# The opening of the first feed-forward product in a two-layer trunk: four sums instead of five, other work moved behind them

## The chip, the cores and the metric

The kernel runs on one core of one Trainium2 chip. The metric is device microseconds of one execution. Of the kernel before, three runs are known: 1134.08, 1134.33 and 1135.26 us, median 1134.33 us. One more execution was profiled: 1136.75 us, of which 1135.0 us are the profiled span and 1.75 us lie around it. Engines are called as the profile calls them: PE (TensorE matmuls), DVE (VectorE), ACT (ScalarE), POOL (GpSimd) and SP (SyncE, which issues most transfers).

## The reference

The input x has 512 tokens of 1024 features. Two layers follow, then a last normalization:

```python
h = rmsnorm(x, attn_norm[l])
proj = einsum('bsd,de->bse', h, w_in[l])        # 1024 -> 3072
... stick-breaking attention on one half, differential attention on the other ...
x = x + einsum('bse,ed->bsd', mixed, w_o[l])    # 1024 -> 1024
h = rmsnorm(x, mlp_norm[l])
u = square(relu(einsum('bsd,df->bsf', h, w_ff1[l])))   # 1024 -> 4096
x = x + einsum('bsf,fd->bsd', u, w_ff2[l])             # 4096 -> 1024
```

All is float32. The change lies mainly in `einsum(h, w_ff1[l])`, the first feed-forward product.

## The kernel before, in words

**Split numbers.** Every float32 operand of a product is split into a high part that TensorE takes exactly (ACT copies it with rounding: `whi`, `h_hi`, `T_hi`, `Ah`) and a low part, the rest (DVE subtracts: `wlo`, `h_lo`, `T_lo`, `Al`). A product is three matmuls: high by high, high by low, low by high (`three`, lines 289 to 294). So each weight tile of 128x1024 costs one ACT and one DVE instruction ("a split", lines 127 and 128), and each is used by 24 matmuls of 256 columns in the feed-forward stage.

**Feed-forward stage.** Each layer has four groups of 1024 of the 4096 hidden features. For both products a group uses a scheme with seven block products in place of eight. In the first product the blocks of h are two halves of the features by two halves of the tokens (`lo_t`, `hi_t`). The seven kinds are taken in the order `1, 2, 5, 6, 7, 3, 4` (`HALVES`), each for two column blocks c = 0, 1. Kinds 1, 2 and 3 use h as it is. Kinds 5, 6, 7 and 4 use sums of h's blocks. These four sums are made once per layer by `opening` (lines 852 to 866), in place in the two scaled copies of h (`hxs`), and split into `T_hi` and `T_lo`. All four groups use them.

The weights of kinds 5, 6, 7 and 3 are sums too. They are made partly by DMAs that add onto a tile, and partly on DVE by `sum1` (line 827, rows named `q<-q,q`), the "raw sums": "y" before kind 6, "z" before kind 3.

**PSUM.** Kinds 1, 6, 7 and 4 of a column block go one after the other into one bank (spot "a"), each added onto what stands there; kinds 5 and 3 share another ("b"). So before kind 7 starts to add, ACT must have copied the bank after kind 6 (`F`, line 949), and before kind 4, after kind 7 (line 951). `tap` makes these copies, adds on DVE (lines 946, 952, 957), and "bends" the finished hidden features: relu and square, two ACT instructions each (line 941), put off until the next product has been issued.

**Second product.** Its seven forms (`11, 21, x1, ...`) use the hidden features of the group and sums of them. `roll` splits one: `Ah` on ACT, `Al` on DVE. The first is rolled ("11") behind kind 2, the next ("21") behind kind 4.

**What sets the order.** A scheduler places instructions on each engine, but a chain of manual dependencies (`line`) fixes the order of the listed ACT and DVE instructions as written, for the feed-forward stage. Each engine works in order, so an instruction that waits holds all behind it. `W.next` takes the split tile for the next 24 matmuls and calls for the splits of the tiles up to five ahead. In the attention stage there are only two split tiles in turn, besides a few "homes": tiles in memory that is not yet used, into which some weights can be split early (`at_home`).

**Start of a layer.** Layer 0 begins with the projections d0, d1, w0, d2, d3 and so on. The sum of squares for the norm goes through a reduction (`ms`), a power on POOL (`rcol`) and a broadcast by PE (`rb_a`). Two homes held the weights of d2 (units 6 and 7) in layer 0.

Of the kernel before, what the change touches and what calls it, by code (L numbers as in the profile page):

```python
# [13 lines left out]
ALU = mybir.AluOpType  # L14
# [157 lines left out]
def trunk(ctx, tc, xT, w, w1, w2, gains, gfin, lamv, cos, sin, out):  # L172
    nc = tc.nc
# [115 lines left out]
    def three(pt, a, b, first, last, onto=False):  # L289
        ah, al = a  # L290
        bh, bl = b
        nc.tensor.matmul(pt, ah, bh, start=first, stop=False, skip_group_check=onto)  # L292
        nc.tensor.matmul(pt, ah, bl, start=False, stop=False, skip_group_check=onto)  # L293
        nc.tensor.matmul(pt, al, bh, start=False, stop=last, skip_group_check=onto)  # L294
# [33 lines left out]
    for l in range(L):  # L328
        last = l == L - 1
        with ExitStack() as actx:  # L330
# [25 lines left out]
            if l == 0:  # L356
# [17 lines left out]
                at_home(6, vs_parts)  # L374
            else:
# [5 lines left out]
                for n in (1, 2):  # L381
                    W.do_split(W.used + n)
                    behind(W.last[1], h[1])
# [6 lines left out]
                W.gate = W.used + 6, squares[-1][1], behind  # L390

# [457 lines left out]
            def t_part(k, t):  # L849
                split(T_hi[:, 4 * k : 4 * k + 4, t], T_lo[:, 4 * k : 4 * k + 4, t], hxs[k][:, :, t])  # L850

            def opening(n):
                b12, b11, b22, b21 = (hxs[k][:, :, t] for k in range(2) for t in (lo_t, hi_t))
                if n == 0:
                    nc.vector.tensor_sub(b11, b11, b12)
                    t_part(0, hi_t)
                elif n == 1:
                    nc.vector.tensor_sub(b21, b22, b21)
                    nc.vector.tensor_sub(b12, b22, b12)
                    nc.vector.scalar_tensor_tensor(  # L860
                        out=b22, in0=b22, scalar=-1.0, in1=b11, op0=ALU.mult, op1=ALU.subtract)
                    t_part(1, lo_t)
                elif n == 2:
                    t_part(0, lo_t)
                elif n == 3:
                    nc.vector.tensor_add(b21, b21, b11)
                    t_part(1, hi_t)
# [12 lines left out]
            for g in range(GROUPS):  # L880
                for c in range(GP // 2):
                    then("q", g, "5", c, sum1, "y", g, c)
                    then("q", g, "6", c, sum1, "z", g, c)
# [24 lines left out]
        with ExitStack() as fctx:  # L908
# [163 lines left out]
            for g in range(GROUPS):  # L1072
                end = g == GROUPS - 1
                kinds = iter(("s", "s", "s", "mm", "mm", "o"))
                for q in HALVES:
                    for c in range(GP // 2):
                        if g == 0:
                            opening({("1", 0): 1, ("2", 0): 2, ("2", 1): 3}.get((q, c)))
# [6 lines left out]
                        for i in range(2):  # L1085
                            for cc in range(4):
                                three(pt[:, 256 * i : 256 * i + 256], wpair(u, 4 * i + cc), mover(q, cc),
                                      q in "125" and i == cc == 0, i == 1 and cc == 3, q not in "125")
# [158 lines left out]
```

## Time and profile before

| what | value |
| --- | --- |
| runs, median (lowest to highest) | 1134.33 us (1134.08 to 1135.26) |
| profiled execution: its time, its span | 1136.75 us, 1135.0 us |
| granted TensorE clock, mean | 0.994 |
| PE busy | 98% of the span |
| DVE busy | 82% |
| ACT busy | 63% |
| POOL busy | 15% |
| DMA | 162 GB/s mean |

A row of the timeline gives the start of an instruction in us, its duration, the engine, the line, the operation, what it writes and reads with sizes, and in brackets the idle time before it and what ended it. The row of a wait gives the total, the number of times and the longest. Rows of a stretch give busy time per engine (instructions), the granted clock (PEclk) and the DMA's share. Matmuls are pipelined: a start follows the one before by less than the duration shown.

### The profile page before, as it was taken

How to read it: one execution, taken by the hardware profiler on the slowest of the kernel's cores; microseconds unless marked ns; L12 is line 12 of the kernel's file. 1: busy time of each engine (PE TensorE's matmuls, PEld its weight loads, DVE VectorE, ACT ScalarE, POOL GpSimd, SP SyncE). 2: the span in 40 equal slices, each digit the busy share in tenths (PEclk: the TensorE clock that was granted, in tenths of full speed). 3: DMA queues.
4: the chain of work that ended last, by engine and by line, in shares of the span. 5: the costliest groups of instructions: out<-in, count | busy, mean ns of one | idle time of the engine just before them, and what ended most of it. 6: DMA issues, size and time to landing. Idle time of an engine off the chain costs nothing.

```text
span 1135.0 us, 18049 instructions
## 1 busy us (share of the span) xinstructions
PE 1116.2 (98%) x6834; PEld 998.1 (88%) x6834; DVE 929.2 (82%) x1238; ACT 711.1 (63%) x1120; POOL 174.5 (15%) x257
## 2 busy tenths in 40 slices
PE   9999999998999999999999999999999999999997
PEld 6889989898889899899888898888988998998986
DVE  7898778897788887878888876887977888878787
ACT  7456666676667566567545566665676666565575
POOL 0001432110210110111100024231101101102012
PEclk9999999998999999999999999999999999999999
DMA  7664453255887876885645743524577777859766
GB/s 257 198 173 125 113 148 101 84 151 174 181 189 201 169 194 211 173 212 139 126 130 155 192 118 112 159 83 136 107 226 162 170 222 161 204 155 194 178 128 151
DMA packets 60471, 183.39 MB, mean 162 GB/s; under 512 B 7521, under 2 KB 8545, under 8 KB 60385
## 3 DMA queue, kind: packets, MB, share of 16 engines
q1 hardware_dynamic: 46272, 131.62, 36.6%
q0 software_dynamic: 13824, 50.34, 25.2%
q8 instruction: 54, 0.88, 0.3%
q10 hardware_dynamic: 288, 0.28, 0.1%
q14 instruction: 33, 0.26, 0.1%
HBM read 154.95 MB, written 2.10 MB: 138 GB/s over the span
## 4 chain that ended last, share of the span: by engine, by line
PE 83%; DVE 8%; ACT 3%; DMA 2%; issue 2%; POOL 1%; SPq 0%; POOLq 0%; ACTq 0%; DVEq 0%
PE f L292 8%; PE f L293 8%; PE f L294 8%; PE x L294 2%; PE x L293 2%; PE x L292 2%; DVE wlo L128 2%; PE wo L292 2%; PE wo L293 2%; PE wo L294 2%; DMA q<-in_w 1%; ACT whi L127 1%; DMA raw<-in_w 1%; PE T0s L591 1%; PE T1s L591 1%
## 5 line engine op out<-in xcount | busy, mean ns | idle before, releaser
L128 DVE TENSOR_TENSOR wlo<-q,whi 128x1024 fp32r<-128x1024 f32 x184 | 223.5, 1220 | 24.9 <-ACT whi L127 24.4
L127 ACT ACTIVATE whi<-q 128x1024 fp32r<-128x1024 f32 x184 | 190.3, 1052 | 51.3 <-DMA q<-in_w 23.8
L292 PE MATMUL f<-T_hi,whi 128*128 128x256 f32 x512 | 147.6, 288 | 6.1 <-ACT F L949 6.1
L293 PE MATMUL f<-T_lo,whi 128*128 128x256 f32 x512 | 146.7, 286 | 0.0
L294 PE MATMUL f<-T_hi,wlo 128*128 128x256 f32 x512 | 146.6, 286 | 0.0
L841 POOL DMA_DIRECT2D q<-in_w x64 | 56.2, 912 | 374.1 <-DVE wlo L128 354.2
L292 PE MATMUL f<-h_hi,whi 128*128 128x256 f32 x384 | 108.9, 284 | 0.6 <-ACT whi L127 0.6
L293 PE MATMUL f<-h_lo,whi 128*128 128x256 f32 x384 | 108.7, 283 | 0.0
L294 PE MATMUL f<-h_hi,wlo 128*128 128x256 f32 x384 | 108.6, 283 | 0.0
L292 PEld LDWEIGHTS f<-T_hi,whi 128*128 128x128 f32 x512 | 100.1, 196 | 6.5 <-ACT F L949 6.5
L293 PEld LDWEIGHTS f<-T_lo,whi 128*128 128x128 f32 x512 | 100.1, 196 | 0.0
L294 PEld LDWEIGHTS f<-T_hi,wlo 128*128 128x128 f32 x512 | 100.1, 196 | 0.0
L941 ACT ACTIVATE F<-F 128x512 f32<-128x512 f32 x112 | 70.4, 628 | 21.8 <-DVE F L946 19.8
L128 DVE TENSOR_TENSOR wlo<-raw,whi 128x1024 fp32r<-128x1024 f32 (+1 forms) x62 | 72.1, 1173 | 4.7 <-ACT whi L127 4.7
L292 PEld LDWEIGHTS f<-h_hi,whi 128*128 128x128 f32 x384 | 73.7, 192 | 1.3 <-ACT whi L127 1.0
L293 PEld LDWEIGHTS f<-h_lo,whi 128*128 128x128 f32 x384 | 73.7, 192 | 0.3
L294 PEld LDWEIGHTS f<-h_hi,wlo 128*128 128x128 f32 x384 | 73.7, 192 | 0.1
L127 ACT ACTIVATE whi<-raw 128x1024 fp32r<-128x1024 f32 (+1 forms) x62 | 59.9, 975 | 19.7 <-PE wo L293 3.8
L240 ACT ACTIVATE Ahx<-F 128x1024 fp32r<-128x1024 f32 x32 | 33.9, 1060 | 55.9 <-PE x L293 24.3
L240 DVE TENSOR_TENSOR Alx<-F,Ahx 128x1024 fp32r<-128x1024 f32 x32 | 39.2, 1225 | 12.1 <-ACT Ahx L240 12.1
L240 DVE TENSOR_TENSOR Al<-F,Ah 128x1024 fp32r<-128x1024 f32 x24 | 29.4, 1225 | 19.9 <-ACT Ah L240 19.7
L524 POOL TENSOR_TENSOR sig1s<-sig1s,C1s 128x128 f32<-128x128 f32 (+3 forms) x32 | 26.1, 817 | 70.5 <-DVE C1s L521 53.0
(960 smaller groups left out, 3298.1 us busy)
## 6 DMA issues: line engine op xcount, KB each, us to landing
q<-in_w SPq DMA_DIRECT2D x100, 512.0 KB, 4.8
q<-in_w POOLq DMA_DIRECT2D x84, 512.0 KB, 6.6
raw<-in_w SPq DMA_DIRECT2D x62, 512.0 KB, 4.1
yw<-in_w SPq DMA_DIRECT2D x12, 512.0 KB, 4.6
yw<-in_w POOLq DMA_DIRECT2D x12, 512.0 KB, 5.9
cs<-in_w SPq DMA_DIRECT2D x8, 512.0 KB, 8.1
ww<-in_w SPq DMA_DIRECT2D x8, 512.0 KB, 3.8
x<-in_xT SPq DMA_DIRECT2D x8, 256.0 KB, 4.2
```

What stands on the lines that cost most here:

```text
L127: h = nc.scalar.activation(hi[:, a:b], raw[:, a:b], AF.Copy)
L128: self.last = h, nc.vector.tensor_tensor(out=lo[:, a:b], in0=raw[:, a:b], in1=hi[:, a:b].bitcast(F32), op=ALU.subtract)
L240: return nc.scalar.activation(hi, src, AF.Copy), nc.vector.tensor_tensor(out=lo, in0=src, in1=hi.bitcast(F32), op=ALU.subtract)
L292: nc.tensor.matmul(pt, ah, bh, start=first, stop=False, skip_group_check=onto)
L293: nc.tensor.matmul(pt, ah, bl, start=False, stop=False, skip_group_check=onto)
L294: nc.tensor.matmul(pt, al, bh, start=False, stop=last, skip_group_check=onto)
L524: nc.gpsimd.tensor_mul(sig[:, 0:wd], sig[:, 0:wd], C[:, 1 : wd + 1])
L591: nc.tensor.transpose(pt[:, n * P : (n + 1) * P], u["w"][qi][:, kb * P : (kb + 1) * P], ident)
L841: paced(nc.gpsimd.dma_start(t, quad(g, q, c), accum_op=ALU.add))
L941: nc.scalar.activation(o, o if i is None else i, fn, scale=by)))
```

## The change: what it does

1. `opening` makes the same four sums by four operations in place of five, each from the one before it. The second is issued ahead of kind 2, the third ahead of kind 5, the fourth (kind 4's) ahead of kind 3. All are now in the ordered chain (`line`), their splits too.
2. In the first group of a layer the raw sums "z" come behind the splits of kind 7's weights, not of kind 6's, and the first `roll` comes behind kind 7, not kind 2.
3. TensorE's order is pinned in the first product: each unit's first matmul comes after the last of the unit before.
4. Layer 0 loses the two homes of d2's weights, so these are split in the common two tiles. In layer 1's start one weight split comes behind the sum of squares.

```diff
     def three(pt, a, b, first, last, onto=False):
-        nc.tensor.matmul(pt, ah, bh, start=first, stop=False, skip_group_check=onto)
-        nc.tensor.matmul(pt, ah, bl, start=False, stop=False, skip_group_check=onto)
-        nc.tensor.matmul(pt, al, bh, start=False, stop=last, skip_group_check=onto)
+        return (nc.tensor.matmul(pt, ah, bh, start=first, stop=False, skip_group_check=onto),
+                nc.tensor.matmul(pt, ah, bl, start=False, stop=False, skip_group_check=onto),
+                nc.tensor.matmul(pt, al, bh, start=False, stop=last, skip_group_check=onto))
...
                 constants(a2)
-                at_home(6, vs_parts)
...
-                for n in (1, 2):
-                    W.do_split(W.used + n)
-                    behind(W.last[1], h[1])
+                W.do_split(W.used + 1)
+                behind(W.last[1], h[1])
                 squares = [add_sq(c, n == 0, tt, nc.vector) for n, c in enumerate(CAME)]
...
                 W.gate = W.used + 6, squares[-1][1], behind
+                W.do_split(W.used + 2)
...
-            def t_part(k, t):
-                split(T_hi[:, 4 * k : 4 * k + 4, t], T_lo[:, 4 * k : 4 * k + 4, t], hxs[k][:, :, t])
-
             def opening(n):
                 b12, b11, b22, b21 = (hxs[k][:, :, t] for k in range(2) for t in (lo_t, hi_t))
                 if n == 0:
-                    nc.vector.tensor_sub(b11, b11, b12)
-                    t_part(0, hi_t)
-                elif n == 1:
-                    nc.vector.tensor_sub(b21, b22, b21)
-                    nc.vector.tensor_sub(b12, b22, b12)
-                    nc.vector.scalar_tensor_tensor(
-                        out=b22, in0=b22, scalar=-1.0, in1=b11, op0=ALU.mult, op1=ALU.subtract)
-                    t_part(1, lo_t)
-                elif n == 2:
-                    t_part(0, lo_t)
-                elif n == 3:
-                    nc.vector.tensor_add(b21, b21, b11)
-                    t_part(1, hi_t)
+                    line(v=nc.vector.tensor_sub(b12, b11, b12))
+                else:
+                    o, i = ((b22, b12), (b11, b11), (b21, b21))[n - 1]
+                    line(v=nc.vector.scalar_tensor_tensor(
+                        out=o, in0=b22, scalar=-1.0, in1=i, op0=ALU.mult, op1=ALU.subtract))
+                src, k, t = ((b12, 0, hi_t), (b22, 1, lo_t), (b11, 0, lo_t), (b21, 1, hi_t))[n]
+                line(*split(T_hi[:, 4 * k : 4 * k + 4, t], T_lo[:, 4 * k : 4 * k + 4, t], src))
...
-                    then("q", g, "6", c, sum1, "z", g, c)
+                    then("q", g, "6" if g else "7", c, sum1, "z", g, c)
...
-                        if g == 0:
-                            opening({("1", 0): 1, ("2", 0): 2, ("2", 1): 3}.get((q, c)))
+                        n = {("2", 0): 1, ("5", 0): 2, ("3", 0): 3}.get((q, c))
+                        if g == 0 and n:
+                            opening(n)
...
-                                three(pt[:, 256 * i : 256 * i + 256], wpair(u, 4 * i + cc), mover(q, cc),
-                                      q in "125" and i == cc == 0, i == 1 and cc == 3, q not in "125")
+                                ops = three(pt[:, 256 * i : 256 * i + 256], wpair(u, 4 * i + cc), mover(q, cc),
+                                            q in "125" and i == cc == 0, i == 1 and cc == 3, q not in "125")
+                                if i == cc == 0 and (q, c) != ("1", 0):
+                                    behind(ops[0], pe_end)
+                        pe_end = ops[2]
...
-                                "2": lambda: line(*roll("11")),
+                                "27"[g == 0]: lambda: line(*roll("11")),
```

The order in which the instructions stand on an engine, at three places. First DVE in layer 0's first group, around the sums of h's halves (`hx0mdl`, `hx0mdh` hold them; `q<-q,q` are raw sums, `F<-F,f` the adds behind kind 2, one for each column block). Before:

```order
L860 SCALAR_TENSOR_TENSOR hx0mdl<-hx0mdl,hx0mdh 128x4x256
L827 TENSOR_TENSOR q_0_2667<-q_0_2667,q_0_2669 128x1024
L240 TENSOR_TENSOR T_lo_2673<-hx0mdh,T_hi_2672 128x4x256
L240 TENSOR_TENSOR T_lo_2673<-hx0mdl,T_hi_2672 128x4x256
L128 TENSOR_TENSOR wlo_2943<-q_0_2666,whi_2942 128x1024
L866 TENSOR_TENSOR hx0mdl<-hx0mdl,hx0mdh 128x4x256
L827 TENSOR_TENSOR q_0_2666<-q_0_2666,q_0_2670 128x1024
L946 TENSOR_TENSOR F_2675<-F_2675,f_2947 128x512
L240 TENSOR_TENSOR T_lo_2673<-hx0mdl,T_hi_2672 128x4x256
L128 TENSOR_TENSOR wlo_2977<-q_0_2667,whi_2976 128x1024
L827 TENSOR_TENSOR q_0_2667<-q_0_2667,q_0_2671 128x1024
L946 TENSOR_TENSOR F_2675<-F_2675,f_2983 128x512
```

After the change, from the second raw sum "y" on:

```order
L826 TENSOR_TENSOR q_0_2671<-q_0_2671,q_0_2673 128x1024
L854 SCALAR_TENSOR_TENSOR hx0mdl<-hx0mdl,hx0mdh 128x4x256
L240 TENSOR_TENSOR T_lo_2677<-hx0mdl,T_hi_2676 128x4x256
L128 TENSOR_TENSOR wlo_2943<-q_0_2670,whi_2942 128x1024
L936 TENSOR_TENSOR F_2679<-F_2679,f_2946 128x512
L128 TENSOR_TENSOR wlo_2973<-q_0_2671,whi_2972 128x1024
L936 TENSOR_TENSOR F_2679<-F_2679,f_2978 128x512
L854 SCALAR_TENSOR_TENSOR hx0mdh<-hx0mdl,hx0mdh 128x4x256
L240 TENSOR_TENSOR T_lo_2677<-hx0mdh,T_hi_2676 128x4x256
L128 TENSOR_TENSOR wlo_3008<-q_0_2672,whi_3007 128x1024
L826 TENSOR_TENSOR q_0_2670<-q_0_2670,q_0_2674 128x1024
L128 TENSOR_TENSOR wlo_3043<-q_0_2673,whi_3042 128x1024
```

Both adds into `F` behind kind 2 now stand ahead of the third sum, its `T_lo` and the raw sums "z". From the first sum of halves to the second of these adds there are now two sums in place of five, two `T_lo` in place of four, and two raw sums in place of four: seven operations of 1024 elements fewer. ACT's order follows (`T_hi`, bends, `whi`).

Second, DVE in the same group from the second add of kind 7 (`F<-F,f`, the first row) towards the low part of form "21" (`Al` of row L240). Before:

```order
L952 TENSOR_TENSOR F_2676<-F_2676,f_3054 128x512
L128 TENSOR_TENSOR wlo_3202<-q_0_2666,whi_3201 128x1024
L957 TENSOR_TENSOR F_2674<-F_2674,f_3022 128x512
L128 TENSOR_TENSOR wlo_3235<-q_0_2667,whi_3234 128x1024
L957 TENSOR_TENSOR F_2674<-F_2674,f_3054 128x512
L128 TENSOR_TENSOR wlo_3268<-q_0_2668,whi_3267 128x1024
L974 TENSOR_TENSOR F_2865<-F_2676,F_2674 128x1024
L975 TENSOR_TENSOR F_2674<-F_2675,F_2674 128x1024
L970 SCALAR_TENSOR_TENSOR F_2675<-F_2865,F_2675 128x1024
L128 TENSOR_TENSOR wlo_3302<-q_0_2669,whi_3301 128x1024
L240 TENSOR_TENSOR Al_3335<-F_2677,Ah_3334 128x1024
```

After the change:

```order
L942 TENSOR_TENSOR F_2680<-F_2680,f_3050 128x512
L854 SCALAR_TENSOR_TENSOR hx0mdl<-hx0mdl 128x4x256
L240 TENSOR_TENSOR T_lo_2677<-hx0mdl,T_hi_2676 128x4x256
L128 TENSOR_TENSOR wlo_3201<-q_0_2670,whi_3200 128x1024
L240 TENSOR_TENSOR Al_3209<-F_2679,Ah_3208 128x1024
L947 TENSOR_TENSOR F_2678<-F_2678,f_3017 128x512
L128 TENSOR_TENSOR wlo_3238<-q_0_2671,whi_3237 128x1024
L947 TENSOR_TENSOR F_2678<-F_2678,f_3050 128x512
L128 TENSOR_TENSOR wlo_3271<-q_0_2672,whi_3270 128x1024
L964 TENSOR_TENSOR F_2869<-F_2680,F_2678 128x1024
```

The fourth sum, its `T_lo` and the low part `Al` of form "11" have come into this stretch; the rows down to `Al` of form "21" follow as before. On PE the scheduler has put two matmuls of the second bank of form "21" ahead of the first one that reads its `Al`.

Third, DVE at layer 0's start, from the reduction for the norm (`ms`) to the scaling of the cosine table (`cs`). Before:

```order
L275 TENSOR_REDUCE ms<-rs_a_299 128x4
L128 TENSOR_TENSOR wlo_378<-raw_211,whi_377 128x1024
L323 TENSOR_TENSOR nlam<-lam_ex 128x1 x2
L277 TENSOR_SCALAR ms<-ms 128x4
L324 TENSOR_SCALAR nlam<-nlam 128x1 x2
L128 TENSOR_TENSOR vs_142<-raw_321,vs_142 128x1024
L128 TENSOR_TENSOR vs_142<-raw_381,vs_142 128x1024
L757 TENSOR_TENSOR cs<-cs,ssq 128x512
L758 TENSOR_TENSOR cs<-cs,ssq 128x512
```

After the change:

```order
L275 TENSOR_REDUCE ms<-rs_a_299 128x4
L323 TENSOR_TENSOR nlam<-lam_ex 128x1 x2
L277 TENSOR_SCALAR ms<-ms 128x4
L324 TENSOR_SCALAR nlam<-nlam 128x1 x2
L128 TENSOR_TENSOR wlo_378<-raw_211,whi_377 128x1024
L756 TENSOR_TENSOR cs<-cs,ssq 128x512
L757 TENSOR_TENSOR cs<-cs,ssq 128x512
```

The split of a w0 weight stands behind `ms<-ms`, and the two splits of d2's weights (`vs`, the homes) have left the place; they now stand where the first two later weight splits stood, in the middle of the attention's work.

## The prediction

> **What bounds the kernel now.** I read the page first, then the waits of PE, then PE's timeline where the longest waits lie.
>
> ```profile
> PE 1116.2 (98%) x6834; PEld 998.1 (88%) x6834; DVE 929.2 (82%) x1238; ACT 711.1 (63%) x1120; POOL 174.5 (15%) x257
> ```
>
> PE is the bound, and the change takes no matmul away. It can only win where PE stands still or runs slowly. The waits of PE (total us, times, longest):
>
> ```profile
> PE f L292 <- ACT F L949: 6.1, 2, 3.7
> ...
> PE rs_a L274 <- DVE ssq L254: 0.5, 1, 0.5
> PE rb_a L286 <- POOL rcol L280: 0.5, 1, 0.5
> ```
>
> The first is more than all the others that the change can touch: once in each layer, kind 7's first matmul waits until ACT has copied kind 6's sums out of the bank. PE's timeline there, layer 0 and layer 1:
>
> ```profile
> 265.47 0.28 PE L294 MATMUL f<-T_hi,wlo 128*128 128x256 f32 x1
> 269.43 0.58 PE L292 MATMUL f<-T_hi,whi 128*128 128x256 f32 x1 [3.68 <-ACT F L949]
> ...
> 274.91 0.28 PE L293 MATMUL f<-T_lo,whi 128*128 128x256 f32 x1
> ```
>
> ```profile
> 827.59 0.28 PE L294 MATMUL f<-T_hi,wlo 128*128 128x256 f32 x1
> 830.31 0.39 PE L292 MATMUL f<-T_hi,whi 128*128 128x256 f32 x1 [2.44 <-ACT F L949]
> ...
> 834.78 0.28 PE L292 MATMUL f<-T_hi,whi 128*128 128x256 f32 x1
> 834.90 0.28 PE L293 MATMUL f<-T_lo,whi 128*128 128x256 f32 x1
> ```
>
> At full speed these matmuls start 0.12 us apart (834.78 to 834.90). From 265.47 to 274.91 lie 26 steps (the first row, then 25 from 269.43 on): 9.44 us instead of 3.12, so 6.32 us are lost, of which 3.68 are standing and 2.64 slow running. From 827.59 to 834.78 lie 25 steps: 7.19 instead of 3.00, 4.19 lost, 2.44 standing and 1.75 slow. The slow part is the clock, as the stretches show (us, PE, PEld, DVE, ACT, POOL, then the granted clock, DMA share and GB/s):
>
> ```profile
> 20.00:30.00 10.00, 9.53 (x48) 7.70 (x47) 8.92 (x21) 4.08 (x6) 2.05 (x1) 1.00 0.62 196
> 265.00:275.00 10.00, 6.32 (x33) 6.12 (x32) 6.58 (x6) 6.74 (x10) 0.00 (x0) 0.66 0.78 282
> 830.00:840.00 10.00, 9.69 (x68) 9.69 (x69) 6.38 (x7) 6.82 (x10) 0.00 (x0) 0.83 0.90 352
> ```
>
> It fell to 0.66 and 0.83 on the mean behind the two long stops, and stayed at 1.00 where PE stood for 0.47 us (the first stretch, 10.00 less 9.53). The two places cost 10.51 us together.
>
> The Trainium skill (TensorE: Matmul & The Clock Gate, Part 1: The HAM clock gate) says that the clock is halved after an idle window of about 3.4 us, and comes back after about as long of steady work. Layer 1's stop of 2.44 us is shorter than that window and the clock fell all the same, so here the row decides and not the Trainium skill. By the Trainium skill alone layer 1 would give back 2.44 us and not 4.19, and the change 1.75 us less.
>
> **Why the copy is late.** ACT's timeline, layer 0:
>
> ```profile
> 253.09 1.06 ACT L240 ACTIVATE T_hi<-hx0mdl 128x1024 fp32r<-128x1024 f32 x1 [2.35 <-DVE hx0mdl L860]
> ...
> 264.62 1.30 ACT L941 ACTIVATE F<-F 128x512 f32<-128x512 f32 x2 [1.88 <-DVE F L946]
> 265.95 1.06 ACT L240 ACTIVATE Ah<-F 128x1024 fp32r<-128x1024 f32 x1
> 266.92 1.99 ACT L127 ACTIVATE whi<-q 128x1024 fp32r<-128x1024 f32 x2
> 268.81 0.56 ACT L949 COPY F<-f 128x512 f32<-128x512 f32 x1
> ```
>
> The copy (268.81) is held by nothing of its own: kind 6's first block was complete a whole unit (24 matmuls, 2.88 us) before 265.59. It stands behind two `whi`, the first roll's `Ah` and kind 2's bend, and the bend waits for DVE's second add into `F`. DVE's timeline, and its busy time from the first sum of halves to that add:
>
> ```profile
> 251.83 1.22 DVE L860 SCALAR_TENSOR_TENSOR hx0mdl<-hx0mdl,hx0mdh 128x1024 f32<-128x1024 f32 x1
> 252.97 1.22 DVE L827 TENSOR_TENSOR q<-q,q 128x1024 f32<-128x1024 f32 x1
> ...
> 259.78 0.68 DVE L946 TENSOR_TENSOR F<-F,f 128x512 f32<-128x512 f32 x1
> 260.38 1.22 DVE L240 TENSOR_TENSOR T_lo<-hx0mdl,T_hi 128x1024 fp32r<-128x1024 f32 x1
> ...
> 263.91 0.68 DVE L946 TENSOR_TENSOR F<-F,f 128x512 f32<-128x512 f32 x1
> ```
>
> ```profile
> 237.30:264.60 27.30, 26.11 (x28) 1.00 0.40 72
> 278.48:293.01 14.53, 11.55 (x11) 1.00 0.73 177
> ```
>
> DVE is busy 26.11 of 27.30 us (first row): it is the bound of this stretch, and PE only feels it at the end. Its operations of 1024 elements follow each other every 1.14 us (251.83 to 252.97), those of 512 every 0.60 (259.78 to 260.38), and SCALAR_TENSOR_TENSOR takes the same 1.22 us as TENSOR_TENSOR, so the new form of three sums costs nothing extra.
>
> **The change part by part: kind 7's wait.** Seven operations of 1024 leave this stretch (three sums, two `T_lo`, two raw sums): 7 x 1.14 = 7.98 us. One new gap replaces the old idle 1.19 us (27.30 less 26.11): `T_lo` now stands straight behind its sum and waits for `T_hi` on ACT, 1.06 us and a handover, some 1.2. So the second add comes at about 263.91 - 7.98 = 255.9; PE has its sums by 265.59 - 4 x 2.88 = 254.1. From there to the copy, DVE has the add 0.6, the third sum 1.14, the gap 1.2, `T_lo` 1.14, a weight split 1.14 and the first raw sum "z" 1.22, which ends at 262.3; then ACT makes the `whi` that reads this raw sum, about 1.0, and the copy 0.56, which ends at 263.9. PE wants it at 265.59. The wait is gone with 1.7 us to spare; a slip of that size would still cost nothing. In layer 1 the same instructions stand with a shorter wait, so I take it as gone too: -10.51 us. Pinning PE's order adds no instruction, and PE already took these units in this order: nothing.
>
> **What is late next.** The moved work comes back behind kind 7. The tight place is form "21", which needs `Al` of its hidden features. The second stretch quoted above is that of DVE from kind 7's second add to the end of this `Al`; its ends, PE's first use, and a late transfer on the way:
>
> ```profile
> 278.48 0.69 DVE L952 TENSOR_TENSOR F<-F,f 128x512 f32<-128x512 f32 x1 [0.72 <-ACT F L951]
> ...
> 291.78 1.23 DVE L240 TENSOR_TENSOR Al<-F,Ah 128x1024 fp32r<-128x1024 f32 x1 [1.02 <-ACT Ah L240]
> ```
>
> ```profile
> 295.11 0.39 PE L294 MATMUL 21000_3367<-whi,Al 128*128 128x512 f32 x1
> ```
>
> ```profile
> 279.34 1.06 ACT L127 ACTIVATE whi<-q 128x1024 fp32r<-128x1024 f32 x1 [0.89 <-DMA q<-in_w]
> ```
>
> PE will come 6.32 us earlier, at 288.8, and two matmuls put ahead give it 0.45: 289.2. The add at 278.48 hangs on PE and moves with it, to 272.2. Into its 14.53 us come the fourth sum 1.14, the round trip to ACT 1.2, its `T_lo` 1.14 and form 11's `Al` 1.14: 4.6. The stretch has 2.98 us idle (14.53 less 11.55). If all is absorbed, `Al` is ready at 272.2 + 14.53 + 4.6 - 3.0 = 288.3 and costs nothing; if none, at 291.3 and PE stops for 2.1 us. The gap of 1.02 waits for `Ah`, which hangs on PE and will be early by comparison, and the late `whi` at 279.34 has its transfer asked for behind a weight split that also moves forward; so most of the idle time is absorbed. I take 0.5 us in each layer, at full clock as after the 0.47 us stop: +1.0, between 0 and 2 x (2.1 + 1.75) = 7.7 with the slow running of layer 1 behind each.
>
> **The starts of the layers.** At layer 0's start three weight splits no longer stand ahead of the norm's small operations and the scaling of the cosine table: the 0.47 us at `rb_a` should go. At layer 1's start one split of 1.14 leaves the sum of squares' way: most of the 0.47 at `rs_a` goes. Together -0.8, between -0.94 and 0. Against it, d2's weights are split in the middle of attention. In layer 0 the place that d2's first split takes on DVE held d3's, and PE came to d2's first low part here:
>
> ```profile
> 40.08 1.22 DVE L128 TENSOR_TENSOR wlo<-raw,whi 128x1024 fp32r<-128x1024 f32 x1
> ```
>
> ```profile
> 41.74 0.39 PE L294 MATMUL p0d2q<-h_hi,vs 128*128 128x512 f32 x1
> ```
>
> ```profile
> 48.11 0.39 PE L292 MATMUL p0d2k<-h_hi,vs 128*128 128x512 f32 x1
> ```
>
> It ends at 41.30, 0.44 us before PE wants it, and the raw loads of later weights are issued later on SP, between the moves of d2's heads. I take +0.2; nothing at the lower end, the slow rival below at the upper.
>
> **Sum.** -10.51 + 1.0 - 0.8 + 0.2 = -10.1 us. The span goes from 1135.0 to 1124.9 and the profiled execution's 1136.75 to 1126.65. That execution was 2.42 us above the median of the runs; I take the same difference from the median: 1134.33 - 10.1 = 1124.2 us.
>
> **The rivals.**
>
> *The stop moves to form "21".* For it: DVE and ACT work in order, PE is earlier by 6 us and the deferred work of 4.6 us lies exactly there. Against: 2.98 us of idle time there, and 2.1 us between the end of `Al` (293.02) and PE's use (295.11) before. With 2.1 us standing and the slow clock behind it in both layers: 1134.33 - 10.51 - 0.8 + 0.2 + 7.7 = 1130.9. By the Trainium skill's idle window (TensorE: Matmul & The Clock Gate, Part 1: The HAM clock gate) a stop of 2.1 us leaves the clock full, and the time would be 1127.4. Layer 1's stop of 2.44 us speaks for the price with the slow clock.
>
> *The change does not do what it says.* The `whi` ahead of the copy now reads the raw sum "z". If DVE is 3 us later than my walk (a raw tile to which a DMA adds, landing late), the copy is late again by some 1.3 us in each layer, and with the slow clock 1.75 more: 2 x 3.05 = 6.1 given back, 1130.3. At more than 4 us it would be near no change.
>
> *Layer 0 turns slow.* Without homes, d2 and d3 (four tiles) go through two tiles in turn. A tile comes free when PE is done with it; PE then has one other tile of 24 matmuls: d2's first takes it 6.4 us from the third matmul (41.74) to d2's second (48.11), heads included. If DVE's queue or the raw load makes a split later than that, PE waits; this is the point from which it decides. With 2.3 us (1.06 and 1.22, the split laid bare) at each of the four, and 1.75 of slow clock: 4 x 4.05 = 16.2, so 1124.2 - 0.2 + 16.2 = 1140.2, slower than before. Against: the later weights of the stage go through the same two tiles, and PE's list of waits has none of 1 us on them.
>
> **How the numbers follow.** The forecast (1122 to 1127) has 0.65, the stop at form "21" 0.19, the copy still late 0.09, layer 0 slow 0.04, and 0.03 is left for the unnamed, taken as no change. The best case is no stop at "21", both starts gained, nothing lost: 1134.33 - 10.51 - 0.94 = 1122.9; a profiled stop may also be a little shorter than that of an ordinary run, so I go to 1121.8. Upwards the range takes in the first two rivals: 1131.2. About 0.2% (2.3 us) is what a measurement of this kernel can tell from no change. Faster by more than that: 0.65 + 0.19 + 0.07 of the late copy = 0.91. Within it: 0.02 + 0.03 = 0.05. Slower: 0.04.
>
> **What would show it.** Right: PE's wait for the copy of kind 6 is no longer in the list, the clock reads 1.00 at both places, DVE's second add follows kind 2 within some 2 us, and a wait of about half a microsecond for `Al` stands at form "21". Wrong: a wait of 2 us at "21" with a clock below 1; a wait for the copy that has stayed; PE waiting for `whi` or `wlo` between 40 and 75 us in layer 0.

## The result, and the profile after

The changed kernel takes 1127.18 us (median of four runs, 1125.84 to 1128.82); the kernel before 1134.8 us (also four runs, 1134.08 to 1135.48). The ratio is 0.9934, with a 95% interval from 0.9916 to 0.9951: 7.5 us less, between 5.6 and 9.5. Two more comparisons of the same pair, told below, gave 0.9936 and 0.9924. The forecast was 1124.2 us, 10.1 less. The direction and the mechanism came as forecast; the size was some 2.5 us too large. Part of that lies in the main step (the slow running was costed from one execution), part in the price of form "21".

The profiled execution of the changed kernel took 1125.84 us, 10.9 less than the profiled one of before (1136.75). It is the fastest of the four runs, and 1136.75 lies above all four runs of before, so this pair shows more than the medians do. The page of the changed kernel, engines:

```profile
PE 1112.8 (99%) x6834; PEld 994.4 (88%) x6834; DVE 926.5 (82%) x1236; ACT 711.6 (63%) x1120; POOL 174.5 (16%) x257
```

PE's waits in the changed kernel (total us, times, longest):

```profile
PE 21000_3370 L294 <- DVE Al L240: 0.4, 1, 0.4
...
PE rs_a L274 <- DVE ssq L254: 0.3, 1, 0.3
PE 21100_9090 L294 <- DVE Al L240: 0.2, 1, 0.2
```

The wait for the copy `F` (6.1 us in two stops) is gone, and so is that at `rb_a`. New are two short stops for `Al` at form "21", one in each layer. The kernel's first group of layer 0 as a whole, from PE's first matmul of its first product to the first of the next group, before and after (PE's timelines):

```profile
242.56 0.28 PE L292 MATMUL f<-h_hi,whi 128*128 128x256 f32 x1
...
322.45 0.28 PE L292 MATMUL f<-h_hi,whi 128*128 128x256 f32 x1
```

```profile
242.39 0.28 PE L292 MATMUL f<-h_hi,whi 128*128 128x256 f32 x1
...
316.72 0.28 PE L292 MATMUL f<-h_hi,whi 128*128 128x256 f32 x1
```

That is 79.89 us before and 74.33 after. In layer 1, read in the same way, it is 78.47 and 74.02. So 10.0 of this pair's 10.9 us lie in the two groups in which the prediction looked for them. The stretches in which kind 7 starts, layer 0 and layer 1 (us, PE, PEld, DVE, ACT, POOL, then the granted clock, DMA share and GB/s):

```profile
262.00:272.00 10.00, 10.00 (x85) 10.00 (x85) 8.36 (x8) 7.46 (x11) 0.00 (x0) 1.00 0.89 317
...
820.00:830.00 10.00, 10.00 (x86) 10.00 (x85) 7.94 (x8) 6.24 (x9) 0.00 (x0) 1.00 0.99 363
```

PE is busy for the whole of both, at full clock. The walk of the prediction can be followed in DVE's and ACT's timelines of the changed kernel, layer 0:

```profile
256.16 0.68 DVE L936 TENSOR_TENSOR F<-F,f 128x512 f32<-128x512 f32 x1
...
259.10 1.23 DVE L240 TENSOR_TENSOR T_lo<-hx0mdh,T_hi 128x1024 fp32r<-128x1024 f32 x1 [1.12 <-ACT T_hi L240]
...
261.38 1.22 DVE L826 TENSOR_TENSOR q<-q,q 128x1024 f32<-128x1024 f32 x1
```

```profile
262.69 1.06 ACT L127 ACTIVATE whi<-q 128x1024 fp32r<-128x1024 f32 x1 [0.54 <-DVE q L826]
263.66 0.57 ACT L939 COPY F<-f 128x512 f32<-128x512 f32 x1
```

The second add came at 256.16 (forecast 255.9), the new gap at `T_lo` was 1.12 us (1.2), the raw sum "z" ended at 262.60 (262.3) and the copy at 264.23 (263.9). PE did not have to wait for it.

### The profile page after: what moved, and what is told of

It is laid out like the page before. It is cut to its first block, busy times and chain, and to the rows that moved or that the text cites. A ratio compares the mean times of both kernels' runs of the same rounds, so it can differ in the third digit from the quotient of the medians.

```text
span 1124.1 us, 18043 instructions
## 1 busy us (share of the span) xinstructions
PE 1112.8 (99%) x6834; PEld 994.4 (88%) x6834; DVE 926.5 (82%) x1236; ACT 711.6 (63%) x1120; POOL 174.5 (16%) x257
## 4 chain that ended last, share of the span: by engine, by line
PE 85%; DVE 7%; ACT 3%; issue 2%; DMA 1%; POOL 1%; SPq 0%; POOLq 0%; DVEq 0%; ACTq 0%
PE f L292 8%; PE f L293 8%; PE f L294 8%; PE x L293 3%; PE x L294 3%; PE x L292 3%; PE wo L292 2%; DVE wlo L128 2%; PE wo L294 2%; PE wo L293 2%; PE T0s L590 1%; DMA q<-in_w 1%; PE T1s L590 1%; PE v0w L292 1%; PE v1w L292 1%
## 5 line engine op out<-in xcount | busy, mean ns | idle before, releaser
L128 DVE TENSOR_TENSOR wlo<-raw,whi 128x1024 fp32r<-128x1024 f32 (+1 forms) x64 | 74.5, 1173 | 5.1 <-ACT whi L127 5.1
L240 ACT ACTIVATE Ahx<-F 128x1024 fp32r<-128x1024 f32 x32 | 34.0, 1061 | 55.1 <-PE x L293 24.3
L240 DVE TENSOR_TENSOR Alx<-F,Ahx 128x1024 fp32r<-128x1024 f32 x32 | 39.2, 1224 | 7.8 <-ACT Ahx L240 7.8
L240 DVE TENSOR_TENSOR Al<-F,Ah 128x1024 fp32r<-128x1024 f32 x24 | 29.4, 1224 | 16.8 <-ACT Ah L240 16.8
L240 ACT ACTIVATE Ah<-F 128x1024 fp32r<-128x1024 f32 x24 | 25.4, 1059 | 19.3 <-issue 15.0
```

The source lines that it names most:

```text
L128: self.last = h, nc.vector.tensor_tensor(out=lo[:, a:b], in0=raw[:, a:b], in1=hi[:, a:b].bitcast(F32), op=ALU.subtract)
L240: return nc.scalar.activation(hi, src, AF.Copy), nc.vector.tensor_tensor(out=lo, in0=src, in1=hi.bitcast(F32), op=ALU.subtract)
```

## The experiments

Each kernel is compared with the kernel before on the same chip; the runs of one table row shared that chip with the rows of the same letter. The medians of before were 1135.4 us (e), 1135.31 (f) and 1136.66 (g).

| run | what it is | median us | ratio to before, 95% interval |
| --- | --- | --- | --- |
| e1 | the changed kernel again | 1128.74 | 0.9936 (0.9924 to 0.9948) |
| e2 | before, raw sums and first roll later | 1129.62 | 0.9949 (0.9937 to 0.9962) |
| e3 | changed, raw sums at the old place | 1130.16 | 0.9955 (0.9941 to 0.9969) |
| e4 | before, changed starts of the layers | 1135.16 | 0.9996 (0.9988 to 1.0005) |
| f1 | before, raw sums later | 1127.44 | 0.9933 (0.9921 to 0.9946) |
| f2 | before, first roll later | 1132.04 | 0.9973 (0.9964 to 0.9982) |
| f3 | changed, fewer transfers | 1127.39 | 0.9927 (0.9915 to 0.9940) |
| f4 | before, fewer transfers | 1134.22 | 0.9987 (0.9978 to 0.9996) |
| g1 | changed, `Al` of "21" one place sooner | 1127.41 | 0.9922 (0.9907 to 0.9937) |
| g2 | before, raw sums later and changed starts | 1127.53 | 0.9920 (0.9905 to 0.9935) |
| g3 | the changed kernel once more | 1127.74 | 0.9924 (0.9910 to 0.9937) |

### Which part of the change takes the stop away

**e1, the changed kernel again**, as the measure for the others of its letter.

> The changed kernel itself, timed in more rounds and profiled once more. If the forecast's sum holds for ordinary runs, the gain over the kernel before is 10.1 us; the four runs so far say 7.6 us at the median with an interval of 5.6 to 9.5 us. Theory: the two stops at kind 7's first matmul and the slow clock behind them are gone in every execution, and the rest of the difference to 10.1 is that ordinary runs of before lose less at these stops than the profiled one did (its time was 2.4 us above their median). Rival: the changed kernel has a stop of its own, of 2 to 3 us, in some executions only; then its runs spread over 3 us while those of before spread over 1.5, and a second profile may show it at form 21 or in layer 0's attention.

The gain is there again: 0.9936, 6.7 us between the medians. Its runs spread over 3.3 us and those of before over 4.3 (1.5 was expected of them), so the difference in spread by which the rival would show is not there. Its profiled execution took 1126.6 us and had one stop more, at the start of group 1 (PE's timeline):

```profile
317.62 0.39 PE L292 MATMUL f<-h_hi,whi 128*128 128x256 f32 x1 [1.07 <-ACT whi L127]
```

**e2, two lines of the change on the kernel before**; opening, pin and starts as before.

```diff
-                    then("q", g, "6", c, sum1, "z", g, c)
+                    then("q", g, "6" if g else "7", c, sum1, "z", g, c)
...
-                                "2": lambda: line(*roll("11")),
+                                "27"[g == 0]: lambda: line(*roll("11")),
```

> Only the raw sums z and the first roll come later in the first group; the five sums of halves, the order pin and the starts are those of before. Theory (the bend that waits for DVE's queue, and the roll's Ah that stands ahead of the copy on ACT): two raw sums leave DVE's stretch (2 x 1.14 = 2.3 us) and Ah leaves ACT's (1.06 us), so the copy comes 3.3 us earlier; the stop of 3.68 us in layer 0 falls to about 0.3 and that of 2.44 us in layer 1 to 0, the clock stays full, and some 9 us are gained, nearly all. Rival (the sums of halves and their splits are what held the second add): the five sums still stand there, the second add comes at most 2.3 us earlier, stops of 1.4 and 0.2 us remain with slow running behind the first, and 5 to 7 us are gained.

0.9949: more than three quarters of the gain, with the old five sums of halves in their old place. PE's waits in this run:

```profile
PE 11001_3340 L292 <- ACT F L941: 1.0, 1, 1.0
...
PE f L292 <- ACT F L949: 0.4, 1, 0.4
```

The copy is 0.4 us late in layer 0 alone, in place of 3.7 and 2.4. So these are the stops of the theory, and the sums of halves need not go for it; but the gain, 5.8 us between the medians, is not the theory's 9 and lies where the rival had it. New is a stop of 1.0 at form "11", which takes part of the rest and to which we come back.

**e3, the whole change but for the raw sums**, which stay behind kind 6's splits.

```diff
-                    then("q", g, "6" if g else "7", c, sum1, "z", g, c)
+                    then("q", g, "6", c, sum1, "z", g, c)
```

> The whole change, but the raw sums z of the first group stand where they stood, behind the splits of kind 6's weights. Theory: five operations instead of seven leave the stretch ahead of the second add (5.7 us instead of 8.0). The copy is then late by 0 to 0.8 us, no slow clock, and about 8 us are gained, 1 to 2 less than with the whole change. Rival (the raw sums z are the item that counts, since they stand between kind 6's splits and the second add): 2.3 us later in both layers, stops of 1 us or more at kind 7 with slow running, and 5 us or less are gained.

0.9955, 5.2 us between the medians, 1.4 less than the whole change and not the 8 us that were expected. There is a short wait for the copy in each layer:

```profile
PE f L292 <- ACT F L939: 0.9, 2, 0.6
```

So the stops also shrink, to 0.6 us and less, without the raw sums' move, when operations of the sums of halves and the roll go instead. No single kind of them has to go: it is the length of the queue.

**f1, one line: the raw sums later** (the first line of e2's diff, on the kernel before).

> The kernel before with one line of the change: in the first group the raw sums z come behind the splits of kind 7's weights. Theory (DVE's queue): in the kernel before the two raw sums, 1.14 us each, stand ahead of DVE's second add behind kind 2 (263.91 us); without them it comes 2.3 us sooner or more, the bend and the roll's Ah follow at once, and ACT has time for Ah (0.97 us) while it waits for the first raw sum, as it stood idle for 1.01 us there in the run with both lines. So the stop at kind 7 falls from 3.7 to 0.4 us and in layer 1 from 2.4 to under 0.3, the second column block may stop for 0.4 more; the clock stays at 1.00. Against about 1135.2 us: 1128.5 to 1130.5. Rival (ACT's queue): the roll's Ah and the two whi hold the copy, and the raw sums only part of it: a stop of 1.4 us stays, time 1131 to 1133.

0.9933, 1127.44 us: this line alone gives the whole gain, more than its own theory had (1128.5 to 1130.5). DVE, then ACT, in layer 0 of this run:

```profile
260.44 0.68 DVE L946 TENSOR_TENSOR F<-F,f 128x512 f32<-128x512 f32 x1
```

```profile
262.69 1.06 ACT L240 ACTIVATE Ah<-F 128x1024 fp32r<-128x1024 f32 x1
263.66 2.02 ACT L127 ACTIVATE whi<-q 128x1024 fp32r<-128x1024 f32 x2
265.58 0.57 ACT L949 COPY F<-f 128x512 f32<-128x512 f32 x1
```

The second add comes 3.47 us sooner than in the kernel before (260.44 against 263.91): two raw sums of 1.14 have gone, and one `T_lo` now stands behind the add (3 x 1.14 = 3.42). The copy stands 3.23 us sooner, though `Ah` is still ahead of it: the rival, that ACT's queue with `Ah` holds the copy, fell. What is left of PE's stops stands in layer 0 alone, twice for 0.2 us (the theory had 0.4 for each of the two column blocks):

```profile
266.20 0.39 PE L292 MATMUL f<-T_hi,whi 128*128 128x256 f32 x1 [0.24 <-ACT F L949]
...
269.55 0.39 PE L292 MATMUL f<-T_hi,whi 128*128 128x256 f32 x1 [0.21 <-ACT F L949]
```

**f2, the other line alone: the first roll later** (the second line of e2's diff).

> The kernel before with the other line alone: the first roll (11) comes behind kind 7. Theory (DVE's queue): the second add stays where it was (263.9 us), so only Ah (0.97 us) leaves ACT's way: the stops go from 3.68 to about 2.7 us and from 2.44 to about 1.5. What the clock then does is open: in the kernel before a stop of 2.44 us was followed by slow running that cost 1.75. If a stop of 1.5 us leaves the clock at 1.00, the time is about 1135.2 - 1.94 - 0.5 - 1.75 + 0.5 = 1131.5; if both stops still slow it, 1133. Rival (ACT's queue): the roll is the main cause, both stops under 1 us, time 1128.5 to 1130.5.

0.9973, 3.3 us less than before between the medians. PE's two stops and the granted clock over them:

```profile
267.49 0.39 PE L292 MATMUL f<-T_hi,whi 128*128 128x256 f32 x1 [2.11 <-ACT F L949]
...
825.55 0.39 PE L292 MATMUL f<-T_hi,whi 128*128 128x256 f32 x1 [1.35 <-ACT F L949]
```

```profile
262.00:272.00 10.00, 7.89 (x66) 7.69 (x65) 8.38 (x8) 7.36 (x10) 0.00 (x0) 1.00 0.59 208
...
825.00:835.00 10.00, 9.45 (x78) 9.45 (x79) 6.53 (x7) 6.17 (x10) 0.00 (x0) 1.00 0.98 391
```

The stops are 2.11 and 1.35 us (expected about 2.7 and 1.5), and **the clock stays at 1.00 behind both** in this execution. So of the two mechanisms, the theory's is the one: the stops shrink by 1.6 and 1.1 us and stay. DVE's second add stood at 263.06 here,

```profile
263.06 0.68 DVE L946 TENSOR_TENSOR F<-F,f 128x512 f32<-128x512 f32 x1
```

0.85 sooner than in the profile of before, so the first stop is shorter than `Ah`'s 0.97 alone would make it. Against the gain stand two new stops at form "21":

```profile
PE 21000_3367 L294 <- DVE Al L240: 0.5, 1, 0.5
PE 21100_9088 L294 <- DVE Al L240: 0.5, 1, 0.5
```

f1, in which the roll stays behind kind 2, has none in layer 0 and one of 0.2 in layer 1. The late roll is thus what brings most of this price with it.

### What the change costs elsewhere

**e4, the changed starts of the layers alone**, on the kernel before.

```diff
-                at_home(6, vs_parts)
...
-                for n in (1, 2):
-                    W.do_split(W.used + n)
-                    behind(W.last[1], h[1])
+                W.do_split(W.used + 1)
+                behind(W.last[1], h[1])
...
                 W.gate = W.used + 6, squares[-1][1], behind
+                W.do_split(W.used + 2)
```

> The kernel before with the changed starts of the layers alone (no homes for d2's weights in layer 0, one weight split behind the sum of squares in layer 1). The forecast's terms are -0.8 and +0.2: 0.6 us faster, which five rounds can hardly tell from nothing; in the profile the waits of 0.5 us at rb_a and rs_a shrink to 0 and at most 0.3 and no wait for whi or wlo comes up in layer 0's attention. Rival (the two tiles in turn hold up d2 and d3): waits of 1 us or more there, and slower.

0.9996: between 1.4 us less and 0.6 more. The wait at `rb_a`, 0.2 to 0.7 us in the five profiles with the old start, is no longer in the list here, nor in any profile with the new one. That at `rs_a` went from 0.5 to 0.3. One that the profile of before does not have stands in layer 0's attention, where a moved head lands late:

```profile
PE S0d L502 <- DMA st0d2q<-hl0d2k: 0.4, 1, 0.4
...
PE rs_a L274 <- DVE ssq L254: 0.3, 1, 0.3
```

What the starts give and what attention takes back is too little to be told from nothing.

**f3 and f4: late weights?** Ordinary runs of the changed kernel are slower than its first profiled one, and e1's profile had a stop for late weights. Both kernels were run without the adding transfers of the second product.

```diff
                 else:
-                    paced(nc.gpsimd.dma_start(t, quad(g, q, c), accum_op=ALU.add))
                     W.raw[_AT[("f", l, g, form, c)]] = t
```

> The changed kernel without the adding transfers of the second feed-forward product: the 64 transfers (8 in each group) that add a second block of weights onto a tile which another transfer filled are left out, so the weights of the forms x1, x2, x3 and x4 lack a term; all instructions of TensorE, VectorE and ScalarE stay. Theory: what ordinary executions of the changed kernel lose beyond the profiled one (1127.2 to 1128.7 against 1125.8) is weights that land late at the end of a group, as the 1.1 us stop at 317.6 us in the second profile. Then the time falls to 1124.5 to 1126, no wait for whi stands in PE's list, and the runs lie closer together (within 1.5 us). Rival: the loss lies elsewhere (attention's moves of heads, the start), and the time stays at 1127 to 1128.7.

> The kernel before without the same 64 transfers. Theory that the two stops gave the late weights time, so that the change uncovers them: layer 0 has no wait for whi to lose, only the 0.58 us at 883 us in layer 1: the time falls by at most 1 us against the kernel before (1134 to 1135), so that the two kernels without these transfers stand 9 to 10 us apart, as forecast, and not 7.5. Rival: late weights cost both kernels alike, and both fall by the same 1 to 3 us, still 7 to 8 us apart. The stops of 3.7 and 2.4 us at kind 7 stay in either case.

The theory fell. f3 stands at 0.9927, among the changed kernel's own three ratios (0.9924 to 0.9936), and f4 is 1.1 us below the kernel before between the medians, so the two are 6.8 us apart and not 9 to 10. No wait for `whi` is in f3's list, and its profiled execution still took 1127.69 us. What it has instead are stops of 0.5 us for `Al` at form "21" in each layer.

**g3, the changed kernel once more**, beside g1 and g2.

> The changed kernel once more, beside the two others on the same chip: 1127.2 to 1128.7 by the two sets so far.

1127.74 us, ratio 0.9924. Its profiled execution took 1128.58 us, 2.7 more than the first one, and shows where 1.2 of them are. ACT, then PE, layer 0:

```profile
276.45 1.06 ACT L127 ACTIVATE whi<-q 128x1024 fp32r<-128x1024 f32 x1 [1.37 <-DMA q<-in_w]
```

```profile
285.39 0.39 PE L294 MATMUL 11000_3342<-whi,Al 128*128 128x512 f32 x1
286.44 0.50 PE L292 MATMUL 11001_3343<-whi,Ah 128*128 128x512 f32 x1 [0.66 <-ACT F L931]
...
291.06 0.49 PE L294 MATMUL 21000_3370<-whi,Al 128*128 128x512 f32 x1 [0.51 <-DVE Al L240]
...
291.85 0.40 PE L294 MATMUL 21000_3370<-whi,Al 128*128 128x512 f32 x1
```

The spacing without a stop, in PE's timeline of the first profile of the changed kernel (ten steps):

```profile
285.68 0.39 PE L293 MATMUL 11001_3343<-wlo,Ah 128*128 128x512 f32 x1
...
287.94 0.39 PE L294 MATMUL 11001_3343<-whi,Al 128*128 128x512 f32 x1
```

A `whi` for form "11" waits 1.37 us for its weights (which come by a transfer that f3 did not leave out). ACT works in order: behind that `whi` stand the bends, and PE stops for a bend at 286.44 and for `Al` at 291.06. From 285.39 to 291.85 lie 20 matmuls, which at 0.227 us each take 4.54 us: 6.46 less 4.54 is 1.92 us lost, though only 1.17 are shown as stops. Behind each stop the next few steps are wider as well. The first profile lost 0.73 here (shown below), which gives the 1.2; the other 1.5 us of the difference lie elsewhere, and most of them stay open. In e2 the corresponding `whi` waited 4.50 us, and its stop at form "11" was the 1.0 us shown above:

```profile
277.42 1.06 ACT L127 ACTIVATE whi<-q 128x1024 fp32r<-128x1024 f32 x1 [4.50 <-DMA q<-in_w]
```

In f1, with the roll at its old place, the same `whi` was late too, and PE has no stop at forms "11" and "21" of layer 0:

```profile
276.90 1.06 ACT L127 ACTIVATE whi<-q 128x1024 fp32r<-128x1024 f32 x1 [2.78 <-DMA q<-in_w]
```

So a late weight alone did not stop PE here; with the late roll in the queue as well (e2, g3) it did.

**g1, `Al` of form "21" sooner:** one subtraction of 1.26 us goes behind it in DVE's queue.

```diff
             def behind_3():
                 line(v=nc.vector.tensor_sub(F[4], F[2], F[0]))
                 line(v=nc.vector.tensor_sub(F[0], F[1], F[0]))
-                less(1, 4, 1)
 
             def behind_4():
                 line(*roll("21"))
+                less(1, 4, 1)
                 less(3, 1, 3)
```

> The changed kernel with one subtraction of hidden features (line 960, 1.26 us) moved from ahead of form 21's Al to behind it, in every group. Theory: the changed kernel's remaining stops of 0.4 to 0.5 us at form 21 are DVE's queue; each costs about 0.8 us of PE's time in layer 0 (289.64 us is 0.56 later than the spacing before it, and the next steps are wider). With Al 1.26 us sooner both are gone and TensorE takes the four opening matmuls of the form in their plain order: about 1.3 us less than the changed kernel beside it, so 1125.5 to 1127.5. Rival: what stops PE there is not Al's place in the queue but Ah on ACT: no change.

No difference from the changed kernel beside it (0.9922 against 0.9924; 1127.41 and 1127.74 us). The rival's forecast held. DVE, then PE, layer 0, in this run:

```profile
287.85 1.23 DVE L240 TENSOR_TENSOR Al<-F,Ah 128x1024 fp32r<-128x1024 f32 x1 [0.71 <-ACT Ah L240]
```

```profile
288.52 0.39 PE L293 MATMUL 21000_3370<-wlo,Ah 128*128 128x512 f32 x1
289.13 0.50 PE L294 MATMUL 21000_3370<-whi,Al 128*128 128x512 f32 x1 [0.22 <-DVE Al L240]
```

`Al` now waits 0.71 us for `Ah` on ACT, so it comes 0.52 sooner (288.37 before the edit), not 1.26. And PE asks for it sooner: it takes the form's matmuls in their plain order, so the two of the second bank that stood ahead of the first use of `Al` no longer give it their 0.45 us. The two cancel nearly; the stops of PE are 0.22 and 0.53 us. DVE's queue and ACT's, which has no idle time between the last bends and this `Ah`, are late within some 0.5 us of each other here, so making one shorter is not enough.

**g2, the raw sums later and the changed starts**, with the old opening and the first roll behind kind 2: an attempt at a version better than both kernels.

> The kernel before with late raw sums and the changed starts of the layers, old opening, first roll behind kind 2. Theory: the raw sums give the whole gain (1127.4 alone), and the starts take out the 0.7 us wait at rb_a and part of the 0.5 at rs_a, against what their moves cost in attention (nothing in the median when tried alone): 1126.3 to 1127.5, thus as fast as the changed kernel or faster, though the new opening and the late roll are left out. Rival: the new opening is worth something after all: this kernel is 1 us or more behind the changed one.

0.9920, 1127.53 us: the same as the changed kernel, with much less of the change. It is not a faster version. The new opening with the first roll at its old place was not tried.

## Why the prediction was right or wrong

**Kind 7's wait (-10.51): the mechanism held; as a price for ordinary runs the size was some 0.9 too large.** The copy was late because DVE's queue ahead of the second add was too long; f1 shows it (two raw sums and one `T_lo` out of the way, and of the stop twice 0.2 us is left), and the changed kernel's rows came within 0.4 us of the walk. In the pair of profiles the price is right: kind 7's stops and the slow running went with all their 10.5 us (PE's first product in this group is 6.31 us shorter in layer 0 and 4.17 in layer 1). What failed is that the slow running, read from one execution, was taken for that of all. In layer 0 of the profile of before, 2.64 us were lost to the clock. f4 has the same stop in the same place; PE's timeline and its stretch:

```profile
265.43 0.28 PE L294 MATMUL f<-T_hi,wlo 128*128 128x256 f32 x1
269.44 0.58 PE L292 MATMUL f<-T_hi,whi 128*128 128x256 f32 x1 [3.74 <-ACT F L948]
...
274.11 0.28 PE L294 MATMUL f<-T_hi,wlo 128*128 128x256 f32 x1
```

```profile
265.00:275.00 10.00, 6.26 (x40) 6.06 (x40) 6.91 (x7) 7.64 (x11) 0.00 (x0) 0.83 0.79 290
```

From 265.43 to 274.11 lie 27 steps: 8.68 us instead of 3.24, so 5.44 lost, of which 1.70 are slow running, at a mean clock of 0.83 and not 0.66. e4 reads the same in that stretch:

```profile
265.00:275.00 10.00, 6.35 (x41) 6.15 (x40) 7.05 (x7) 7.51 (x10) 0.00 (x0) 0.83 0.75 269
```

Layer 1 has a stop of 2.45 us in f4 and 2.44 in e4, as in the profile of before, and read in the same way it cost 4.20 and 4.19. So the two stops are worth about 5.44 + 4.20 = 9.6 us in such an execution, and 10.5 in the one that I costed. The mean granted clock of the runs of the kernel before tells how usual that one is (three chips together):

| mean clock of the run | runs of before | their median us (lowest to highest) |
| --- | --- | --- |
| 0.994 | 11 | 1136.66 (1135.12 to 1137.99) |
| 0.995 | 28 | 1135.34 (1134.07 to 1137.25) |
| 0.996 | 8 | 1135.0 (1133.56 to 1137.51) |
| 0.997 | 2 | 1132.88 (1132.86 to 1132.89) |

The execution that I costed had 0.994, the lowest. The changed kernel had 0.998 or 0.999 in each of 15 runs. A thousandth of the clock over 1135 us is 1.1 us of full speed. So the kernel before loses less to the clock in most of its runs than in the one profiled, and the change can give back no more than that. The clock is not all: runs of one mean clock still lie up to 4 us apart, and what else differs between them is not shown.

**The stop at form "21" (+1.0): right place, too small for ordinary runs.** Forecast: 0.5 us in each layer, at full clock. First profile of the changed kernel, PE, layer 0 and layer 1:

```profile
288.85 0.39 PE L293 MATMUL 21001_3371<-wlo,Ah 128*128 128x512 f32 x1
289.64 0.50 PE L294 MATMUL 21000_3370<-whi,Al 128*128 128x512 f32 x1 [0.41 <-DVE Al L240]
...
291.85 0.40 PE L294 MATMUL 21000_3370<-whi,Al 128*128 128x512 f32 x1
```

```profile
844.53 0.39 PE L293 MATMUL 21101_9091<-wlo,Ah 128*128 128x512 f32 x1
845.10 0.50 PE L294 MATMUL 21100_9090<-whi,Al 128*128 128x512 f32 x1 [0.18 <-DVE Al L240]
...
845.90 0.39 PE L294 MATMUL 21100_9090<-whi,Al 128*128 128x512 f32 x1
```

Ten steps take 3.00 us instead of 2.27, four take 1.37 instead of 0.91: 0.73 + 0.46 = 1.2 us. That is the good case. In g3 layer 0 lost 1.92, and its stop of 0.21 in layer 1 costs about what that of 0.18 does here: 2.4. DVE in the first profile of the changed kernel shows what the walk left out, in the `Al` of form "11" (first row) and of form "21":

```profile
278.25 1.23 DVE L240 TENSOR_TENSOR Al<-F,Ah 128x1024 fp32r<-128x1024 f32 x1 [0.91 <-ACT Ah L240]
...
288.37 1.22 DVE L240 TENSOR_TENSOR Al<-F,Ah 128x1024 fp32r<-128x1024 f32 x1
```

Most of the old idle time was absorbed, as forecast: the second `Al` no longer waits for its `Ah`. But form "11"'s `Al`, counted at 1.14, brings a round trip to ACT of its own, 0.91 us. With some 0.6 us of old idle time left, form "21"'s `Al` ends at 289.59 and not at 288.3. PE is ready for it 0.227 behind 288.85, at 289.1, as forecast (289.2). Two more things were not in the working. A stop costs more than the wait list shows, 0.3 us more for each here. And late weights for form "11", which the kernel before could bear (its `whi` waited 0.89 us with no stop of PE behind it), now reach PE through ACT's bends; that part varies from one execution to the next. A stop of 0.5 us did not touch the clock, as forecast.

**The starts (-0.8) and attention (+0.2).** The wait at `rb_a` went, as forecast, and part of that at `rs_a`. Together e4 puts these parts at -0.2 us by the medians, between -1.4 and +0.6; the 0.4 us at `S0d` in e4's profile is the sort of price meant by the +0.2. -0.6 is inside the interval and is neither shown nor refuted.

**Pinning PE's order (nothing).** In the profiles of both kernels PE takes the matmuls of the first product in the same order, as the prediction said. The changed kernel without the pin was not run, so that it is worth nothing is argued only.

**The sum again, with what was measured:** -9.6, +1.2 to +2.4, -0.2: -8.6 to -7.4, against differences of the medians of 7.6, 6.7 and 8.9 us. The first groups of the two layers together, measured as in the section on the result, say the same without counting steps: 158.36 us in the profile of before, 156.84 in f4 and 156.71 in e4; 148.35, 149.32 and 149.59 in the three profiles of the changed kernel. The pair first profiled gained 10.0 us there, where -10.51 and +1.0 were forecast (0.58 of the 10.0 is a late `whi` of before that the forecast did not count); against f4 and e4 the gain is 7.1 to 8.5. f1 took 148.57, as little as the whole change. So the forecast was right for the one execution that it was read from, 1126.65 forecast and 1125.84 profiled, which is luck in part, since the changed kernel's execution was its fastest; it was wrong to take 10.1 us from the median. The absolute forecast, 1124.2, is 3.0 us too low: 2.5 from the sum, and 0.5 because it started from the median of three runs, 1134.33, where four gave 1134.8.

**The rivals.** The stop moved to form "21" in part: the place was right, the price (7.7) was not, since no stop there came near the 2.1 us for which it was worked out. The late copy and the slow layer 0 did not happen; no wait for `whi` or `wlo` stands in the changed kernel's list.

**The clock.** Behind stops of 2.44, 2.45, 3.65, 3.68 and 3.74 us the clock fell; behind 1.35 and 2.11 us it stayed at 1.00. The Trainium skill (TensorE: Matmul & The Clock Gate, Part 1: The HAM clock gate) puts the idle window at about 3.4 us; the stops of 2.44 and 2.45 disagree with it, as the prediction said. Both stops with a full clock are of one execution, the profile of f2, so a limit between 2.11 and 2.44 us is not shown: the ordinary runs of f2 had mean clocks from 0.997 to 0.999, and in some of them the clock may have fallen. Nor does it fall at the end of a stop: in layer 1 of the profile of before PE resumed at 830.31 and kept its full spacing until 831.25, some 0.9 us, before the steps widened to 0.21.

## What to carry to other kernels

When an engine stops for a copy that is held by nothing of its own, walk back through the queue in which the copy stands, to the engine that feeds that queue, and count the operations there that are not yet needed: here one line that puts two of them behind the tight place gave as much as the whole rewrite. What is moved arrives somewhere: cost the place to which it goes with all engines that queue there, and with the round trip to another engine that each moved operation may bring, and the transfers that will now be waited for. Take the size of a stop's after-effects from more than one profiled execution, since the clock and late transfers differ between them, and do not take a loss read from a slow execution off the median of faster ones.

## What was not expected of the hardware

- A stop of 3.7 us cost 2.64 us of slow running in one execution and 1.70 in another (mean clock over the same stretch 0.66 and 0.83), with the same stop in the same place; over whole runs of the kernel before the mean clock went from 0.994 to 0.997, and the median time from 1136.66 to 1132.88 us with it (the last is the median of two runs).
- A stop of 2.11 us left the clock alone in one execution, where stops of 2.44 and 2.45 in three were each followed by some 1.75 us of loss to slow running, which began up to 0.9 us after PE had resumed.
- A short stop of PE costs more than the idle time shown: 0.41 us idle cost 0.73, 0.18 cost 0.46, at full clock, since the steps next to it are wider (0.35 us from 289.64 to 289.99, against 0.227).
